# Front of a single-layer S5 + SwiGLU kernel: the modulation rows made in four column pieces at four array positions, their two halves turned one at a time, and the context scaled in two steps around them

## The chip, the cores and the metric

The kernel runs on one core of a Trainium2 chip. The metric is the device time of one execution in microseconds (us), as the median of several runs. TensorE is called PE, VectorE DVE, ScalarE ACT, GpSimd POOL, and SyncE, which here only issues transfers, SP.

## The reference

One layer (kind 0) is computed over 1024 latent tokens with 256 context tokens ahead of them, 1024 channels wide, all in fp32. What matters here stands at its start: the modulation vectors are one row of products with `ada_w`, and the normalised tokens are scaled and shifted by them, those of the context (`c_ctx`) by others than those of the latents (`c`).

```python
m_l = split(silu(c) @ ada_w + ada_b, 6); m_c = split(silu(c_ctx) @ ada_w + ada_b, 6)
h_l = rms_norm(x, norm_mix) * (1 + m_l[1]) + m_l[0]
h_c = rms_norm(ctx, norm_mix) * (1 + m_c[1]) + m_c[0]
y_l = s5_mixer(h_c, h_l, ...)     # 64 groups of 16 channels, complex state of 64, both directions
x = x + m_l[2] * y_l
x = x + m_l[5] * swiglu(modulate(rms_norm(x, norm_ffn), m_l[3], m_l[4]))
out = rms_norm(x, norm_final)
```

## The kernel before, in words

The kernel is written for manual scheduling: every engine runs its instructions in the order in which the Python program issues them, and waits for another engine by semaphores that are put in from the tiles' dependences.

The S5 scan works on chunks of 8 tokens. `U` holds the input as 128 partitions (8 tokens x 16 channels) by 64 groups by 160 columns (32 context chunks `Xc`, 128 latent chunks `X`). For 16 half blocks `hb` (8 groups, one direction each) the program makes a weight matrix, turns it on PE and multiplies U by it:

- `bl_make(hb)` makes the two products of a weight (128x1024 each), on POOL for the `hb` listed in `PMUL`, on DVE for the others; `bl_sum(hb)` adds the two, on POOL for `hb` under 4, and by an accumulating transfer that POOL issues (L433) from 4 on; `bl_tr(hb)` turns the sum in eight PE transposes (L443) and copies the result to the buffer `Win` (L446). `hb` 0 is special: DVE makes both products and their sum, and the copy of its turned weight is shared by ACT (L553) and DVE (L555).
- `sums(hb)` multiplies U by the turned weight (L584) and ACT copies the result into the state buffer (L590 to L593); `pair` and `ctx_tree` combine states on DVE and POOL; `lb_dup` (L331 on PE, L332 on ACT) makes the table `LB` from which the weights are made.
- The modulation (shift and scale) is needed by channel, in the partitions of U. `ada1(h, k)` (L199) adds the products of one 128-row tile of `ada_w` into the PSUM tile `prow`, of half h (512 columns of both shift and scale). `mix_rows` (L456, ACT) copies the rows out, `mix_turn` (L460, PE) turns them, `mix_scale` (DVE, by the helpers on L77 and L80) adds the bias and the norm's weight, `mix_sel` (L475, L476, PE) spreads the result over the partitions, `mix_cols` (L481, ACT) copies it out of PSUM.
- With it `u_act` (L497, ACT, one group an instruction) and `u_lat` (DVE, several groups an instruction) modulate the latent columns and `u_ctx` (POOL, two instructions for 8 groups) the context. Ahead of them `rs_lat` and the product with `rcp` apply the norm on DVE.

Half 0 is handled ahead of the loop over `hb`, half 1 inside it (rows at `hb` 3, scale at `hb` 4). SP loads in a fixed order: x, the context, the first B matrices (`bxy`), then eight tiles of `ada_w` for half 0 and eight for half 1. When the 16 half blocks are through and the context's states are joined, the latent scan runs as a chain of small DVE steps (`scan`, a function of its own), and after it come the GLU and the FFN, which are products on PE.

Of the kernel before, what the change touches and what calls it, by code (L numbers as in the profile page):

```python
# [42 lines left out]
def s5_ffn_kernel(tc, a, out):  # L43
# [3 lines left out]
    with ctx:  # L47
# [23 lines left out]
        def bc(ap, axis, n):  # L71
            sh = list(ap.shape)
            sh.insert(axis, n)
            return ap.unsqueeze(axis).to_broadcast(sh)

        def tt(o, x, y, op, eng=V):
            eng.tensor_tensor(out=o, in0=x, in1=y, op=op)  # L77
# [116 lines left out]

        def ada1(h, *ks):
            for k in ks:
                for b in range(2):
                    i = 2 * b + h
                    PE.matmul(prow[32 * i:32 * i + 2], scs[:, k], stage[h][k][:, b], start=k == 0, stop=k == 7, tile_position=(0, 32 * i))  # L199

        for i in range(10):
            src = X[:, 8 * i:8 * i + 8] if i < 8 else ctxT[:, 32 * i - 256:32 * i - 224]
# [125 lines left out]
        def lb_dup(d, i, pt):  # L328
# [2 lines left out]
            PE.matmul(pt, cid[:, d], CP[:, :, i] if d else CP[:, ::-1, i], start=True, stop=True)  # L331
            S.activation(LB[:, i, :, G * d:G * d + G], pt, AF.Copy, scale=sgn[:, 0:1] if i else 1.0)  # L332

        for i in range(2):
            lb_dup(0, i, pw([512]))
        cmul(PW[:, 7:8], PW[:, 3:4])
        ada1(0, *range(3, 8))
        psW.__exit__(None, None, None)
        psW, pW = pool("psV")

# [64 lines left out]
        def bl_make(hb, o2=None):  # L405

            if hb >= 16:
                return
            b, d = bd(hb)
            es = slice(64 * d + 8 * b, 64 * d + 8 * b + 8)  # L410
            for i in range(2):
                l_ = bc((LBP[hb][:, i] if hb in LBP else LB[:, i, :, es]).rearrange("p s g -> p g s"), 3, HC)
                tt(o2 if i and o2 is not None else bls(hb)[i], bc(BXY[:, b // 2 % 2, i, d, 8 * (b % 2):8 * (b % 2) + 8], 2, T), l_, MUL, E if hb in PMUL else V)
# [38 lines left out]

        r4, mx = view(RA, 74, [4, P]), view(RA, 76, [2, 2, 32])

        def mix_rows():
            S.copy(r4, prow.rearrange("p (m n) -> p m n", m=4))  # L456

        def mix_turn():
            for m in range(4):
                PE.transpose(prow[:, P * m:P * m + P], r4[:, m], ident)  # L460

        def mix_scale(h):

            hs, pt = slice(4 * h, 4 * h + 4), prow.rearrange("p (m n) -> p m n", m=4)
            for r in range(2):
                tt(cb[:, r, :, hs], pt.rearrange("p m (b j q) -> p b j m q", b=2, j=2)[:, :, h, :, r], modb[:, 0:2, hs], ADD)
            stt(cb[:, :, 1, hs], cb[:, :, 1, hs], 1.0, bc(nrm[:, 0, hs], 1, 2), ADD, MUL)
            for r in range(2):
                tt(mx[:, r].rearrange("p b (j g) -> p b j g", g=T), bc(cb[:, r, :, hs], 3, T), bc(bc(msk, 1, 4), 1, 2), MUL)
# [3 lines left out]
        def mix_sel(h):  # L473

            PE.matmul(colp[:, :, 32 * h:32 * h + 32], sel, mx[:, 0], start=True, stop=True)  # L475
            PE.matmul(pcol, sel, mx, start=True, stop=True)  # L476

        def mix_cols(h, eng=V):
            o = cols[:, :, :, 32 * h:32 * h + 32]
            if eng is S:  # L480
                S.copy(o, pcol)  # L481
            else:
                eng.tensor_copy(o, pcol)
# [11 lines left out]
        def u_act(b, n0, n1):  # L495
            for g in range(8 * b + n0, 8 * b + n1):
                S.activation(X[:, g], X[:, g], AF.Identity, bias=cols[:, 0, 0, g:g + 1], scale=cols[:, 0, 1, g:g + 1])  # L497

        def u_lat(b, n0=0):
            gs = slice(8 * b + n0, 8 * b + 8)  # L500
            tt(X[:, gs], X[:, gs], bc(colp[:, 1, gs], 2, P), MUL)
            tt(X[:, gs], X[:, gs], bc(colp[:, 0, gs], 2, P), ADD)
# [36 lines left out]
        lb_psum(0, S)  # L539
        pr0 = pv2()  # L540
        o2 = pr0.rearrange("p j (i s h) -> p (j i) s h", i=4, s=T)
        bl_make(0, o2)
        tt(BL1[0], BL1[0], o2, ADD)
        V.reciprocal(rcp, rsc)
        tt(Xc[:, 0:16], ctxT[:, 0:16], bc(rcp, 1, 16), MUL)
        mix_rows()
        pl1 = pv2()
        lb_dup(1, 0, pl1[:, 0])
        mix_turn()
        mix_scale(0)  # L550
        pt, w_ = bl_tr(0, copy=False)
        mix_sel(0)
        S.copy(w_[:, 0].rearrange("p i n -> p (i n)"), pt[:, 0])  # L553
        mix_cols(0, S)
        V.tensor_copy(w_[:, 1].rearrange("p i n -> p (i n)"), pt[:, 1])  # L555
        u_act(0, 0, 4)
        u_lat(0, 4)
        u_ctx(0)
        lb_dup(1, 1, pl1[:, 1])
        rs_lat(1)  # L560
        bl_tr(1)
# [136 lines left out]
        for hb in range(16):  # L698
            sums(hb)
            ada1(1, *ADA1.get(hb, ()))  # L700
            if hb == 0:
                power8()
            if hb == 3:
                mix_rows()
            for n in BLTR.get(hb, (hb + 2,)):
                if n < 16:
                    bl_tr(n)
            if hb == 3:
                mix_turn()
            if hb == 4:  # L710
                mix_scale(1)
                mix_sel(1)
            if hb in RSL:
                rs_lat(RSL[hb])
            if hb == 4:
                mix_cols(1)
                tq = pA.tile([P, 512], F32, tag="r3", name="tq")
                LQ += [t[:, o_:o_ + 192].rearrange("p (r e) -> p r e", e=G) for t, o_ in ((tq, 0), (tq, 192), (LTb, 256))]
            if hb == 0:
                tt(Xc[:, 16:], ctxT[:, 16:], bc(rcp, 1, G - 16), MUL)  # L720
            if hb == 1:
                powers(0)
            if hb == 2:
                powers(1)
                SY.dma_start(BXY[:, 1], a["bxy"][:, 3])
            if hb in UACT:
                u_act(*UACT[hb])
            if hb in UCTX:
                u_ctx(UCTX[hb])
            if hb >= 1:  # L730
                pair(hb - 1, E if hb - 1 in PPAIR else V)
            if hb == 5:
                powers(2, 3)
            for a_ in CTREE.get(hb, ()):
                ctx_tree(*a_)
            if hb + 6 in (7, 9, 11, 12, 14, 15):
                lb_psum(hb + 6)
            bl_sum(hb + 5)
            bl_make(hb + 6)
            if hb == 3:  # L740
                pw_mul(PW[:, 2:3], PW[:, 0:1], PW[:, 1])
                tt(KD.rearrange("p q g h -> p (q g) h"), bc(pat, 1, 8), bc(dcol, 2, HC), MUL, E)
            if hb == 4:
                pw_mul(PW[:, 4:6], PW[:, 0:2], PW[:, 3])
                pw_mul(PW[:, 6:7], PW[:, 2:3], PW[:, 3])
            if hb in (6, 8):
                pw_full(hb // 2 - 3)
            if hb == 9:
                cs_load(0)
            if hb == 11:  # L750
                V.tensor_copy(LQ[4], SQ[4])
                cs_sign(0)
            for _ in range(CLAT.get(hb, 0)):
                CL0.pop(0)()
            ada_load(ADA2.get(hb, 0))
# [1004 lines left out]
```

## Time and profile before

| | |
|---|---|
| median of 3 runs | 1024.42 us (1023.78 to 1026.05) |
| the profiled execution | 1022.42 us, its span in the trace 1020.6 us |
| granted PE clock, mean | 0.991 |
| busy in the span | PE 961.9, DVE 785.5, POOL 766.5, ACT 436.5 us |

Times in the trace count from the start of the span. A row of the timeline gives the start, the length, the engine, the line of the kernel with its operation, out<-in by the names of the tiles, the shape, how many records of that kind follow each other (xN), and in brackets the idle time of the engine just before with the work that ended it. An fp32 product on PE leaves two records. DVE and ACT records may overlap the one after them by some 0.08 us. Nearly all helpers of DVE and POOL record their work under L77, L80, L84 or L86, so such rows are told apart by tile and shape. A row of the waits gives who waited for whom, the sum in us, how often and the longest.

### The profile page before, as it was taken

The page shows a single profiled execution, that of the slowest core. Times are in us where ns is not written, and L with a number is a line of the kernel's source. Part 1 is how long each engine was busy: PE and PEld are TensorE (multiplying, and loading weights), DVE is VectorE, ACT ScalarE, POOL GpSimd, SP SyncE. Part 2 cuts the span into 40 slices and gives each one's busy share as a digit, 9 for nine tenths or more (in the row PEclk, how much of TensorE's full clock was granted, in tenths as well). Part 3 has the DMA queues.
Part 4 walks back from the last instruction along what each step waited for, and adds up shares of the span by engine and source line. Part 5 has one row for each costly group of instructions (what it writes and reads, how often), then busy time and mean ns, then how long its engine had stood idle before and what let it go on. Part 6 is the DMA issues. An engine that isn't in the chain of part 4 may idle for free. (4 is left out here: it accounts for less than half of the span.)

```text
span 1020.6 us, 18545 instructions
## 1 busy us (share of the span) xinstructions
PE 961.9 (94%) x6988; PEld 771.8 (76%) x6988; DVE 785.5 (77%) x1642; ACT 436.5 (43%) x854; POOL 766.5 (75%) x590
## 2 busy tenths in 40 slices
PE   5987798779999999999999999999999999999996
PEld 1466423668999987878888888888888888888885
DVE  7979799994365777997958768585958778686987
ACT  5477622234454663523334343424343343324337
POOL 5799899991682548979786877778686877777674
PEclk9999999989999999999999999999999999999999
DMA  9764997323612021011212112121212111121205
GB/s 335 276 139 91 298 341 231 91 74 89 227 61 83 2 104 62 22 42 42 83 41 74 39 45 62 42 73 52 73 42 82 39 40 58 42 73 52 73 22 165
DMA packets 48546, 98.95 MB, mean 97 GB/s; under 512 B 4285, under 2 KB 18877, under 8 KB 47177
## 3 DMA queue, kind: packets, MB, share of 16 engines
q1 hardware_dynamic: 43272, 86.64, 25.9%
q0 software_dynamic: 2016, 7.34, 3.8%
q10 hardware_dynamic: 3168, 3.79, 1.1%
q8 instruction: 55, 0.90, 0.4%
q14 instruction: 35, 0.28, 0.1%
HBM read 84.25 MB, written 6.17 MB: 89 GB/s over the span
## 5 line engine op out<-in xcount | busy, mean ns | idle before, releaser
L77 POOL TENSOR_TENSOR c<-rxc,c 128x512 fp32r<-128x512 f32 x128 | 170.0, 1342 | 55.6 <-ACT c L1227 53.7
L1286 PE MATMUL ut<-ra,c 128*128 128x512 f32 x400 | 155.8, 390 | 0.5 <-ACT ra L1227 0.3
L1287 PE MATMUL ut<-ra,c 128*128 128x512 f32 x400 | 155.7, 389 | 0.3 <-DVE ra L77 0.3
L1288 PE MATMUL ut<-ra,c 128*128 128x512 f32 x400 | 155.7, 389 | 0.0
L1227 ACT CAST c<-rxc 128x512 fp32r<-128x512 f32 x128 | 79.0, 622 | 146.4 <-PE xt L1568 51.8
L1568 PE MATMUL xt<-c,c 128*128 128x512 f32 x540 | 129.7, 389 | 0.0
L77 DVE TENSOR_TENSOR ru<-ru,xt 128x1024 f32<-128x1024 f32 x90 | 107.8, 1216 | 12.9 <-PE xt L1568 9.1
L1568 PEld LDWEIGHTS xt<-c,c 128*128 128x128 f32 x540 | 101.4, 188 | 21.0
L77 DVE TENSOR_TENSOR ru<-ut,ru 128x512 f32<-128x512 f32 x98 | 67.2, 686 | 42.4 <-PE ut L1288 36.9
L1286 PEld LDWEIGHTS ut<-ra,c 128*128 128x128 f32 x400 | 75.1, 188 | 16.7 <-ACT ra L1227 0.8
L1287 PEld LDWEIGHTS ut<-ra,c 128*128 128x128 f32 x400 | 75.1, 188 | 16.2 <-issue 0.6
L1288 PEld LDWEIGHTS ut<-ra,c 128*128 128x128 f32 x400 | 75.1, 188 | 15.9 <-POOL c L77 0.3
L77 POOL TENSOR_TENSOR c<-rw,c 128x512 fp32r<-128x512 f32 (+1 forms) x29 | 39.8, 1372 | 37.3 <-ACT c L1227 36.6
L77 POOL TENSOR_TENSOR c<-ru,c 128x512 fp32r<-128x512 f32 (+1 forms) x39 | 58.0, 1487 | 9.3 <-ACT c L1227 4.9
L1288 PE MATMUL ut<-c,c 128*128 128x512 f32 x160 | 62.4, 390 | 1.3 <-POOL c L77 1.3
L1287 PE MATMUL ut<-c,c 128*128 128x512 f32 x160 | 62.3, 389 | 0.0
L1286 PE MATMUL ut<-c,c 128*128 128x512 f32 x160 | 62.2, 389 | 0.0
L77 POOL TENSOR_TENSOR rxc<-rxc 128x512 f32<-128x512 f32 x40 | 60.9, 1523 | 1.6
L1568 PE MATMUL ut<-c,c 128*128 128x512 f32 x216 | 51.9, 389 | 0.0
L584 PE MATMUL pv<-ru,c 128*64 128x160 f32 x512 | 43.7, 312 | 7.3 <-POOL ru L77 2.6
L77 DVE TENSOR_TENSOR pe<-pe,ru 128x256 f32<-128x256 f32 x64 | 27.4, 429 | 29.5 <-ACT pe L1127 17.4
L77 DVE TENSOR_TENSOR ru<-ru,ut 128x512 f32<-128x512 f32 x76 | 47.3, 680 | 0.3
(427 smaller groups left out, 2568.2 us busy)
## 6 DMA issues: line engine op xcount, KB each, us to landing
c<-in_ada_w SPq DMA_DIRECT2D x46, 256.0 KB
rxc<-in_w SPq DMA_DIRECT2D x38, 256.0 KB
rxc<-in_w SPq DMA_DIRECT2D x19, 512.0 KB
ru<-in_w SPq DMA_DIRECT2D x11, 512.0 KB
rw<-in_w SPq DMA_DIRECT2D x11, 512.0 KB
ra<-in_ada_w SPq DMA_DIRECT2D x10, 512.0 KB
ra<-in_ada_w SPq DMA_DIRECT2D x18, 256.0 KB
ru<-in_xT SPq DMA_DIRECT2D x4, 1024.0 KB
```

The source lines that it names most:

```text
L77: eng.tensor_tensor(out=o, in0=x, in1=y, op=op)
L584: PE.matmul(pv[64 * (i % 2):64 * (i % 2) + 64, ri, c0:c0 + 160], w[:, i, 64 * ri:64 * ri + 64], U[:, 8 * b + 4 * j + i], start=True, stop= ...
L1227: S.copy(o[0], x)
L1286: PE.matmul(pu, wh, bh, start=start, stop=False)
L1287: PE.matmul(pu, wh, bl, start=False, stop=False)
L1288: PE.matmul(pu, wl, bh, start=False, stop=stop)
L1568: PE.matmul(pd, w[:, cs_], b, start=j in (1, 2, 4) and n == 0, stop=n == 2, skip_group_check=j not in (1, 2, 4))
```

## The change

Each `ada1` step makes four products of 256 columns at the four column positions of the array, where it made two of 512 columns at two positions; half h of the modulation then lies in columns 256h to 256h + 255 of `prow`, on four rows. So `mix_rows(h)` copies 256 columns and `mix_turn(h)` turns two tiles, where 512 and four were handled for either half. `mix_scale` adds the bias in four instructions of four columns instead of two of eight. The step `ada1(0, 3)` goes ahead of the first `lb_dup`.

Ahead of the loop the order is another one: the reciprocal `rcp` and the context's first 8 groups come before the products of weight 0; the whole modulation of half 0 (rows, turn, scale, spread, copy out, `u_ctx(0)`, `u_act`) comes before `lb_dup(1, 0)` and before the turning of weight 0; the context's groups 8 to 15 are scaled behind `u_act`, and `u_lat(0, 4)` follows them.

```diff
         def ada1(h, *ks):
             for k in ks:
-                for b in range(2):
-                    i = 2 * b + h
-                    PE.matmul(prow[32 * i:32 * i + 2], scs[:, k], stage[h][k][:, b], start=k == 0, stop=k == 7, tile_position=(0, 32 * i))
+                for i in range(4):
+                    b, j = divmod(i, 2)
+                    PE.matmul(prow[32 * i:32 * i + 2, 256 * h:256 * h + 256], scs[:, k], stage[h][k][:, b, 256 * j:256 * j + 256],
+                              start=k == 0, stop=k == 7, tile_position=(0, 32 * i))
...
+        ada1(0, 3)
         for i in range(2):
             lb_dup(0, i, pw([512]))
         cmul(PW[:, 7:8], PW[:, 3:4])
-        ada1(0, *range(3, 8))
+        ada1(0, *range(4, 8))
...
-        def mix_rows():
-            S.copy(r4, prow.rearrange("p (m n) -> p m n", m=4))
+        def mix_rows(h):
+            S.copy(r4[:, 2 * h:2 * h + 2], prow[:, 256 * h:256 * h + 256].rearrange("p (m n) -> p m n", m=2))
-        def mix_turn():
-            for m in range(4):
+        def mix_turn(h):
+            for m in (2 * h, 2 * h + 1):
                 PE.transpose(prow[:, P * m:P * m + P], r4[:, m], ident)
         def mix_scale(h):
-            hs, pt = slice(4 * h, 4 * h + 4), prow.rearrange("p (m n) -> p m n", m=4)
+            hs, pt = slice(4 * h, 4 * h + 4), prow[:, 256 * h:256 * h + 256].rearrange("p (m n) -> p m n", m=2)
             for r in range(2):
-                tt(cb[:, r, :, hs], pt.rearrange("p m (b j q) -> p b j m q", b=2, j=2)[:, :, h, :, r], modb[:, 0:2, hs], ADD)
+                for b in range(2):
+                    tt(cb[:, r, b, hs].rearrange("p (j m) -> p j m", j=2), pt.rearrange("p m (b j q) -> p b j m q", b=2, j=2)[:, b, :, :, r],
+                       modb[:, b, hs].rearrange("p (j m) -> p j m", j=2), ADD)
...
+        V.reciprocal(rcp, rsc)
+        tt(Xc[:, 0:8], ctxT[:, 0:8], bc(rcp, 1, 8), MUL)
         bl_make(0, o2)
         tt(BL1[0], BL1[0], o2, ADD)
-        V.reciprocal(rcp, rsc)
-        tt(Xc[:, 0:16], ctxT[:, 0:16], bc(rcp, 1, 16), MUL)
-        mix_rows()
+        mix_rows(0)
+        mix_turn(0)
+        mix_scale(0)
+        mix_sel(0)
+        mix_cols(0, S)
+        u_ctx(0)
+        u_act(0, 0, 4)
+        tt(Xc[:, 8:16], ctxT[:, 8:16], bc(rcp, 1, 8), MUL)
+        u_lat(0, 4)
         pl1 = pv2()
         lb_dup(1, 0, pl1[:, 0])
-        mix_turn()
-        mix_scale(0)
         pt, w_ = bl_tr(0, copy=False)
-        mix_sel(0)
         S.copy(w_[:, 0].rearrange("p i n -> p (i n)"), pt[:, 0])
-        mix_cols(0, S)
         V.tensor_copy(w_[:, 1].rearrange("p i n -> p (i n)"), pt[:, 1])
-        u_act(0, 0, 4)
-        u_lat(0, 4)
-        u_ctx(0)
         lb_dup(1, 1, pl1[:, 1])
         rs_lat(1)
         bl_tr(1)
```

In the loop, `mix_rows()` and `mix_turn()` at `hb` 3 become `mix_rows(1)` and `mix_turn(1)`.

How the built programs stand there follows for the engines of which the prediction speaks; "waits" names the queues for whose semaphores an instruction waits, DVE its own among them.

On DVE, ahead of the loop, from the sum of weight 0 to the two instructions of `u_lat(0, 4)`, before (`ru` is U, `ltb` holds `rcp` and the spread modulation, `c1` and `c3` hold weights, `pv` is PSUM, `rxa` the context as loaded):

```order
L77 TENSOR_TENSOR c1_64<-c1_64,pv_290 128x1024 [waits DVE_49]
L544 RECIPROCAL ltb_77<-r0_60 128x32
L77 TENSOR_TENSOR ru_62<-rxa_67,ltb_77 128x16x32 [waits DMAHW0_49,DVE_49]
L77 TENSOR_TENSOR ltb_77<-prow_75,r0_60 128x2x4 [waits DVE_49,DMAHW3_49,PE_49,Activation_49]
L77 TENSOR_TENSOR ltb_77<-prow_75,r0_60 128x2x4 [waits DVE_49]
L80 SCALAR_TENSOR_TENSOR ltb_77<-ltb_77,r0_60 128x2x4 [waits DMAHW4_49,DVE_49]
L77 TENSOR_TENSOR ra_61<-ltb_77,r0_60 128x64 [waits DVE_49]
L77 TENSOR_TENSOR ra_61<-ltb_77,r0_60 128x64
L555 COPY c3_66<-pv_309 128x512 [waits DMAHW2_49,Activation_49]
L77 TENSOR_TENSOR ru_62<-ru_62,ltb_77 128x4x128 [waits PE_49]
L77 TENSOR_TENSOR ru_62<-ru_62,ltb_77 128x4x128 [waits DVE_49]
```

And in the changed program, from the same sum on (the reciprocal and the scaling of the context's first 8 groups stand ahead of the two products of weight 0 now):

```order
L77 TENSOR_TENSOR c1_64<-c1_64,pv_306 128x1024 [waits DVE_49]
L77 TENSOR_TENSOR ltb_77<-prow_75,r0_60 128x4 [waits DMAHW3_49,PE_49,Activation_49]
L77 TENSOR_TENSOR ltb_77<-prow_75,r0_60 128x4 [waits DVE_49] x3
L80 SCALAR_TENSOR_TENSOR ltb_77<-ltb_77,r0_60 128x2x4 [waits DMAHW4_49,DVE_49]
L77 TENSOR_TENSOR ra_61<-ltb_77,r0_60 128x64 [waits DVE_49]
L77 TENSOR_TENSOR ra_61<-ltb_77,r0_60 128x64
L77 TENSOR_TENSOR ru_62<-rxa_67,ltb_77 128x8x32 [waits PE_49]
L77 TENSOR_TENSOR ru_62<-ru_62,ltb_77 128x4x128
L77 TENSOR_TENSOR ru_62<-ru_62,ltb_77 128x4x128 [waits DVE_49]
L563 COPY c3_66<-pv_337 128x512 [waits DMAHW2_49,Activation_49]
```

DVE's share of the copy of weight 0 (128x512) moved from ahead of `u_lat(0, 4)` to behind it, and the second half of the context's scaling stands where that copy stood. The copy's wait on ACT is for ACT's share of the same copy (L553, now L562), in both programs.

On ACT, from `lb_psum(0)` to the second `lb_dup(1, ...)`, before:

```order
L426 COPY lbt_78<-c2_65 128x128 [waits Activation_49]
L456 COPY ra_61<-prow_75 128x512 [waits PE_49]
L332 ACTIVATE c2_65<-pv_297 128x8x64 [waits PE_49]
L553 COPY c3_66<-pv_309 128x512 [waits DMAHW2_49,PE_49]
L481 COPY r0_60<-prow_75 128x4x32 [waits DVE_49,PE_49]
L497 ACTIVATE ru_62<-ru_62,r0_60 128x128 [waits Activation_49]
L497 ACTIVATE ru_62<-ru_62,r0_60 128x128 x3
L332 ACTIVATE c2_65<-pv_297,r0_60 128x8x64 [waits PE_49]
```

And in the changed program:

```order
L428 COPY lbt_78<-c2_65 128x128 [waits Activation_49]
L458 COPY ra_61<-prow_75 128x256 [waits PE_49]
L485 COPY r0_60<-prow_75 128x4x32 [waits DVE_49,PE_49]
L501 ACTIVATE ru_62<-ru_62,r0_60 128x128 [waits Activation_49]
L501 ACTIVATE ru_62<-ru_62,r0_60 128x128 x3
L333 ACTIVATE c2_65<-pv_334 128x8x64 [waits PE_49]
L562 COPY c3_66<-pv_337 128x512 [waits DMAHW2_49,PE_49]
L333 ACTIVATE c2_65<-pv_334,r0_60 128x8x64 [waits PE_49]
```

The table's activation (128x8x64) and the copy of weight 0 moved from ahead of `mix_cols` and `u_act` to behind them.

On PE, from the last `ada1` steps of half 0 to the turning of weight 1, before:

```order
L199 MATMUL prow<-ra,r_60 2x512 x4
L331 MATMUL pv<-ra 128x512
L460 MATMUL prow<-r_60,ra 128x128 x4
L443 MATMUL pv<-r_60,c_64 128x128 x8
L475 MATMUL ltb<-ra,r_60 128x2x32
L476 MATMUL prow<-ra,r_60 128x128
L331 MATMUL pv<-ra 128x512
```

And in the changed program:

```order
L199 MATMUL prow<-ra,r_60 2x256 x8
L462 MATMUL prow<-r_60,ra 128x128 x2
L479 MATMUL ltb<-ra,r_60 128x2x32
L480 MATMUL prow<-ra,r_60 128x128
L332 MATMUL pv<-ra 128x512
L445 MATMUL pv<-r_60,c_64 128x128 x8
L332 MATMUL pv<-ra 128x512
```

The turning of weight 0 and the table's product stand behind the spreading products now, so behind DVE's scaling for which those wait.

More of the change, by code (lines that the diff above doesn't have):

```diff
@@ L703, in s5_ffn_kernel @@
             if hb == 3:
-                mix_rows()
+                mix_rows(1)
             for n in BLTR.get(hb, (hb + 2,)):
@@ L708, in s5_ffn_kernel @@
             if hb == 3:
-                mix_turn()
+                mix_turn(1)
             if hb == 4:
```

## The prediction

> **What bounds the kernel now.** I first read the busy time by stage. Columns: stretch and its length, then PE, PE's weight loads, DVE, ACT and POOL busy (records), the granted clock, the share of the DMA engines, GB/s.
>
> ```profile
> 28.66:44.80 16.14, 14.23 (x103) 7.21 (x104) 15.52 (x23) 8.32 (x18) 12.77 (x9) 1.00 0.89 329
> 44.88:101.84 56.96, 48.16 (x480) 35.43 (x477) 50.48 (x117) 41.66 (x92) 55.63 (x62) 0.97 0.55 112
> 127.65:200.00 72.35, 63.43 (x1064) 29.75 (x1056) 72.06 (x403) 19.79 (x42) 69.77 (x46) 0.99 0.72 231
> 300.00:350.00 50.00, 50.00 (x423) 50.00 (x422) 32.68 (x96) 24.39 (x74) 16.51 (x15) 1.00 0.20 64
> ```
>
> The bound changes hands: DVE fills the stretch to 44.8 us (15.52 of 16.14), POOL the next 57 us (55.63 of 56.96), DVE the scan (72.06 of 72.35), PE everything behind it. PE is not the bound where the change works.
>
> Next the waits, of DVE from 9 to 62 us and of POOL from 44.5 to 108 us (who waited for whom, us in all, times, longest); each list is complete.
>
> ```profile
> DVE ltb L77 <- DVE ru L77: 0.2, 1, 0.2
> ...
> POOL c L77 <- DVE c L77: 0.6, 1, 0.6
> POOL c L433 <- POOL c L77: 0.3, 1, 0.3
> ```
>
> So DVE runs from 9 us on with one gap of 0.2 us, and POOL from 44.88 on with one of 0.3. The timeline shows where they meet.
>
> ```profile
> 37.71 2.58 POOL L77 TENSOR_TENSOR ru<-ru,r 128x256 f32<-128x256 f32 x4 [2.28 <-ACT r L481]
> 40.25 4.01 POOL L77 TENSOR_TENSOR c<-c,c 128x1024 f32<-128x1024 f32 x2
> 42.45 2.35 DVE L77 TENSOR_TENSOR c<-c,lbt 128x1024 f32<-128x1024 f32 x2
> 44.88 4.71 POOL L77 TENSOR_TENSOR c<-c,c 128x1024 f32<-128x1024 f32 x2 [0.62 <-DVE c L77]
> ```
>
> DVE's `bl_make(2)` ends at 42.45 + 2.35 = 44.80, and POOL, which had finished `u_ctx` and `bl_make(3)` at 44.26, starts `bl_sum(2)` at 44.88. That is the handover. The other end of POOL's stretch:
>
> ```profile
> 101.84 0.88 POOL L433 DMA_DIRECT2D c<-c  x1
> c<-c POOLq DMA_DIRECT2D x1, 512.0 KB, 7.8
> 109.81 0.96 PE L443 MATMUL pv<-r,c 128*128 128x128 f32 x7 [1.20 <-DMA c<-c]
> 115.04 0.43 DVE L77 TENSOR_TENSOR ltb<-ra,lta 128x256 f32<-128x256 f32 x1 [4.64 <-ACT ra L593]
> 127.65 0.29 DVE L77 TENSOR_TENSOR ltb<-ra,lta 128x128 f32<-128x128 f32 x1
> ```
>
> POOL issues an accumulating transfer at 101.84, it lands 7.8 us later, PE waited 1.20 us for it before it turns that weight, and DVE waited 4.64 us for the states made with it; the scan starts at 127.65. **The chain** is DVE to 44.80, POOL to 101.84, the transfer, PE and ACT, DVE's scan, PE. What moves the end of `bl_make(2)` moves the end of the kernel.
>
> **The change part by part.** *The pieces at four positions* (PE):
>
> ```profile
> 23.11 1.03 PE L199 MATMUL prow<-c,r 128*2 128x512 f32 x4
> 135.36 1.04 PE L531 MATMUL pm<-ra,r 128*2 128x512 f32 x8
> 31.86 0.09 PEld L199 LDWEIGHTS prow<-ra,r 128*2 128x2 f32 x2 [0.34 <-DMA ra<-in_ada_w]
> 33.36 0.59 ACT L456 COPY ra<-prow 128x512 f32<-128x512 f32 x1 [3.41 <-PE prow L199]
> ```
>
> Two products at two positions take 1.03 us from first start to last end; four of the same size at four positions (`ada`, later) take 1.04. So positions run side by side, and a step of four halves should take about half as long. The last tile lands near 31.8 us, so the rows are ready at about 32.4 instead of 33.3, and copy and turning (0.59 for 512 columns, less for 256) are done by 33.5. If the pieces did not run side by side, nothing would come later than now: ready before 35. That matters only if somebody waits, and DVE, which reads the rows next, is not there before 35.1 (below). Worth: **0**. The eight steps of half 1 run in the loop where POOL is the bound: 0.
>
> *DVE up to the scaling:*
>
> ```profile
> 29.64 1.22 DVE L77 TENSOR_TENSOR ru<-ru,ltb 128x1024 f32<-128x1024 f32 x1
> 30.78 1.21 DVE L77 TENSOR_TENSOR c<-c,lbt 128x1024 f32<-128x1024 f32 x1
> 33.17 1.22 DVE L77 TENSOR_TENSOR c<-c,pv 128x1024 f32<-128x1024 f32 x1
> 34.31 0.35 DVE L544 RECIPROCAL ltb<-r 128x32 f32<-128x32 f32 x1
> 34.69 0.69 DVE L77 TENSOR_TENSOR ru<-rxa,ltb 128x512 f32<-128x512 f32 x1
> 35.58 0.38 DVE L77 TENSOR_TENSOR ltb<-prow,r 128x8 f32<-128x8 f32 x2 [0.20 <-DVE ru L77]
> 36.00 0.17 DVE L80 SCALAR_TENSOR_TENSOR ltb<-ltb,r 128x8 f32<-128x8 f32 x1
> 36.21 0.36 DVE L77 TENSOR_TENSOR ra<-ltb,r 128x64 f32<-128x64 f32 x2
> 52.22 0.42 DVE L77 TENSOR_TENSOR lbt<-ra,lta 128x256 f32<-128x256 f32 x1
> ```
>
> `rs_lat(0)` still ends at 30.86. The reciprocal waits for it now: 30.90 to 31.25. The context's first half has 256 elements, for which I take 0.42 from the 128x256 row: to 31.70. The three steps of weight 0 took 30.78 to 34.39, 3.61 us, and overlap what is ahead by 0.08: 31.62 to 35.23. Then the scaling: instructions of four columns are not in the trace; the nearest row is two of eight in 0.38, 0.21 from start to start. I take 0.21 each (bounds: 0.10, if half the columns take half the time, and 0.21, what eight columns take); four make 0.84; with 0.21 and 0.36 behind, from 35.15 to **36.56**. Before it was 36.21 + 0.36 = 36.57, with a gap of 0.20 that goes. So the modulation comes no earlier: half the context moved behind it saves 0.27 us, the gap 0.2, the two added instructions take 0.42 back.
>
> [...]
>
> *From the scaling to `rs_lat(1)`:*
>
> ```profile
> 36.62 0.43 PE L475 MATMUL ltb<-ra,r 128*128 128x64 f32 x2 [0.94 <-DVE ra L77]
> 37.17 1.02 PE L331 MATMUL pv<-ra 128*128 128x512 f32 x2
> 38.03 1.04 PE L443 MATMUL pv<-r,c 128*128 128x128 f32 x8
> 34.41 0.60 ACT L332 ACTIVATE c<-pv 128x512 f32<-128x512 f32 x1 [0.46 <-PE pv L331]
> 35.72 0.59 ACT L553 COPY c<-pv 128x512 f32<-128x512 f32 x1 [0.71 <-PE pv L443]
> 37.37 0.27 ACT L481 COPY r<-prow 128x128 f32<-128x128 f32 x1 [1.07 <-PE prow L476]
> 37.67 1.65 ACT L497 ACTIVATE ru<-ru,r 128x128 f32<-128x128 f32 x4
> 36.48 0.68 DVE L555 COPY c<-pv 128x512 f32<-128x512 f32 x1
> 37.09 1.41 DVE L77 TENSOR_TENSOR ru<-ru,ltb 128x512 f32<-128x512 f32 x2
> ```
>
> Before, DVE's copy (0.68) stood over PE's spreading product (36.62 + 0.43 = 37.05), `u_lat(0, 4)` followed at 37.09 to 38.50, and `rs_lat(1)` began at 38.42. Now:
>
> 1. The context's second half comes first, but waits for the spreading product (the order shows the wait on PE): 37.06 to 37.48. The cover of that wait is gone. `u_lat(0, 4)`: 37.40 to 38.81. That is 0.31 later.
> 2. Then DVE's copy, which waits for ACT's half of it. PE's product and turning (1.02, 1.04, as in the rows) are through near 39.1 and hide. ACT does not: `mix_cols` and `u_act` end at 37.67 + 1.65 = 39.32 as before, and behind them stand now the table (0.60, from 39.23) and the copy (0.59), to about 40.33. DVE's copy runs 40.36 to 41.04, `rs_lat(1)` begins at 40.96.
>
> So 40.96 - 38.42 = **2.5 us later**: 0.3 for the context's half, 1.55 of waiting for ACT, 0.6 for a copy that lay in a shadow. Behind that DVE's instructions to the end of `bl_make(2)` are the same and have no slack: 44.80 becomes 47.3. Queued behind the waiting copy are `rs_lat(1)`, `u_lat(1)` and both `bl_make`; PE's turning of weight 1 waits for it too, hence `sums(0)`.
>
> *POOL.* `u_ctx(0)` starts at 37.65 as now (ACT's `mix_cols` decides), `bl_make(3)` ends at 44.3, and the wait for DVE grows from 0.62 to 3.1 us. `bl_sum(2)` starts at 47.4, 2.5 us late, and POOL's 57 us behind it have nothing to give back. No transfer moves by itself; each follows the engine that issues it.
>
> **The sum:** the execution that was profiled, 1022.42 us (span 1020.6 and 1.8 around it), becomes 1024.9; the median of the runs shown stands 2.0 above it, so I forecast 1024.42 + 2.5 = **1026.9 us**. The shift's own bounds: 2.0 (the four instructions at 0.10, so all that follows 0.44 earlier) to 2.8 (three of ACT's steps without the overlap of 0.08).
>
> **The rivals.**
>
> *Swallowed on the way.* PE wins back up to 4 us in half 1 (eight steps, each half of 1.03), and PE and DVE both wait at the exit (1.20, 4.64). If one of these, not POOL, sets the exit, 1 us or more of the 2.5 is gone: 1024.4 to 1026.3. For it: slack is visible on PE. Against it: both waits are for work that comes from POOL, whose own list of waits is empty.
>
> *Faster: the rows set the pace.* If the path ran through `prow`, the modulation and the context's first sums (ACT's 3.41 us wait for PE, POOL's 2.28 for ACT, are its marks), then the 0.9 us by which the rows are ready sooner and up to 4.1 us for half 1 (eight steps, each half of 1.03) would come off: 1019.4 to 1023.5, say 1021.5. It decides once DVE reaches the scaling before the rows are turned, that is, from 33.5 us instead of 35.1 on. Against it: DVE's only gap there is 0.2 us, on itself.
>
> [...]
>
> *Slower still: the transfers.* The transfer at the exit took 7.8 us, one of the same size at 49.53 us took less:
>
> ```profile
> c<-rxc POOLq DMA_DIRECT2D x1, 512.0 KB, 4.7
> ```
>
> It runs against the later `ada_w` loads. If these come closer to it, up to the difference, 3.1 us, may come on top: 1028 to 1030.
>
> **How the numbers follow.** Forecast 0.58, swallowed 0.24, faster 0.09, slower still 0.09. 0.2% is 2.0 us, about what a measurement of this kernel can tell from no change. Of the forecast's 0.58 I put 0.06 under that bound; with the swallowed case that makes 0.30 for the same, 0.61 for slower, 0.09 for faster. The forecast's own range is 1025.9 to 1027.7 (2.0 to 2.8, and half a us for the medians); 8 in 10 need most of the swallowed case and part of the transfers': 1024.2 to 1028.4.
>
> **What would show it.** Right: DVE idle some 1.5 us ahead of its copy of weight 0, released by ACT's; `bl_make(2)` ending near 47.3; POOL's wait for DVE 3 us instead of 0.6, and the scan's start at 130.2. The `ada1` steps in half the time, with ACT's wait ahead of `mix_rows` shorter by about 0.9, show the first part right whatever the total does. Wrong: a copy on DVE that does not wait for ACT (then 0.9 us late, about 1025.3), or new gaps on POOL behind 47 us while the scan starts at its old time.

## The result, and the profile after

The changed kernel took 1027.18 us in the median of 10 runs (1026.72 to 1028.17), against 1024.43 for the kernel before on the same chip: a ratio of 1.0031, 95% interval 1.0023 to 1.0039, **2.75 us slower**. Measured once more with the experiments below it was 1027.95 against 1023.99, ratio 1.0034 (1.0018 to 1.0050), 3.96 slower. In us the two intervals are 2.4 to 4.0 and 1.8 to 5.1. The forecast was 1026.9. The profiled execution of the changed kernel is the slowest of its 10 runs (1028.17, span 1026.4), that of the kernel before lies 2.0 below its median; so the two traces stand 5.8 us apart, more than the medians.

DVE's timeline of the changed kernel, from the scaling to `bl_make(2)`:

```profile
35.28 0.78 DVE L77 TENSOR_TENSOR ltb<-prow,r 128x4 f32<-128x4 f32 x4
36.09 0.17 DVE L80 SCALAR_TENSOR_TENSOR ltb<-ltb,r 128x8 f32<-128x8 f32 x1
36.30 0.36 DVE L77 TENSOR_TENSOR ra<-ltb,r 128x64 f32<-128x64 f32 x2
37.44 0.42 DVE L77 TENSOR_TENSOR ru<-rxa,ltb 128x256 f32<-128x256 f32 x1 [0.78 <-PE ltb L479]
37.78 1.40 DVE L77 TENSOR_TENSOR ru<-ru,ltb 128x512 f32<-128x512 f32 x2
42.01 0.69 DVE L563 COPY c<-pv 128x512 f32<-128x512 f32 x1 [2.83 <-ACT c L562]
42.62 3.72 DVE L77 TENSOR_TENSOR ru<-ru,ltb 128x1024 f32<-128x1024 f32 x3
...
46.64 2.35 DVE L77 TENSOR_TENSOR c<-c,lbt 128x1024 f32<-128x1024 f32 x2
```

The scaling ends at 36.30 + 0.36 = 36.66 us. Then come the two gaps that were forecast: one for the spreading product (0.78), one for ACT's copy. The second is 2.83 instead of the forecast 1.55, and `bl_make(2)` ends at 46.64 + 2.35 = 48.99 instead of 47.3 (44.80 before). What ACT waited for stands in its timeline:

```profile
32.29 0.37 ACT L458 COPY ra<-prow 128x256 f32<-128x256 f32 x1 [2.38 <-PE prow L199]
...
39.83 0.58 ACT L333 ACTIVATE c<-pv 128x512 f32<-128x512 f32 x1
41.39 0.59 ACT L562 COPY c<-pv 128x512 f32<-128x512 f32 x1 [0.98 <-PE pv L445]
```

ACT was through with the table at 40.41 and stood idle for 0.98 us until PE had turned weight 0. PE's timeline tells why:

```profile
31.61 0.61 PE L199 MATMUL prow<-ra,r 128*2 128x256 f32 x8 [0.70 <-DMA ra<-in_ada_w]
...
36.71 0.69 PE L479 MATMUL ltb<-ra,r 128*128 128x64 f32 x2 [3.56 <-DVE ra L77]
37.20 0.74 PE L480 MATMUL prow<-ra,r 128*128 128x128 f32 x2
37.73 1.91 PE L332 MATMUL pv<-ra 128*128 128x512 f32 x2
39.44 1.91 PE L445 MATMUL pv<-r,c 128*128 128x128 f32 x8
```

After 3.56 us of idle time every product takes 1.6 to 1.9 times what it took before the change: the spreading 0.69 and 0.74 (0.43, 0.44), the table 1.91 (1.02), the turning 1.91 (1.04). It is the clock. The busy time by stage, columns as in the prediction, with the stretches cut where the trace records a change of the clock:

```profile
29.17:32.58 3.41, 1.82 (x28) 0.30 (x20) 3.31 (x5) 1.00 (x3) 3.41 (x2) 1.00 1.04 396
32.58:35.99 3.41, 0.44 (x2) 0.20 (x2) 3.27 (x7) 0.09 (x1) 2.88 (x2) 1.00 1.06 389
35.99:42.82 6.83, 6.11 (x16) 3.64 (x17) 3.12 (x9) 2.98 (x7) 4.35 (x5) 0.50 0.95 351
42.82:46.23 3.41, 3.41 (x41) 2.90 (x40) 3.34 (x3) 2.73 (x5) 2.08 (x2) 1.00 0.02 8
```

The granted clock is 0.50 from 35.99 to 42.82, behind a stretch in which PE was busy 0.44 of 3.41 us. Before the change it was 1.00 through the whole front (until 84 us). POOL, at the handover and at its last transfer but one:

```profile
49.07 4.71 POOL L77 TENSOR_TENSOR c<-c,c 128x1024 f32<-128x1024 f32 x2 [3.23 <-DVE c L77]
106.02 0.88 POOL L435 DMA_DIRECT2D c<-c  x1
```

`bl_sum(2)` starts 4.19 us late, and 57 us later the transfer is issued 4.18 late (101.84 before): POOL gave nothing back. At the exit, the transfer (the last figure is the time to its landing), PE and DVE:

```profile
c<-c POOLq DMA_DIRECT2D x1, 512.0 KB, 8.2
114.32 1.78 PE L445 MATMUL pv<-r,c 128*128 128x128 f32 x8 [1.81 <-DMA c<-c]
120.26 0.43 DVE L77 TENSOR_TENSOR ltb<-ra,lta 128x256 f32<-128x256 f32 x1 [4.63 <-ACT ra L598]
125.86 0.43 DVE L77 TENSOR_TENSOR ltb<-ra,lta 128x256 f32<-128x256 f32 x1 [1.57 <-ACT ra L595]
```

The transfer landed 8.2 us after its issue instead of 7.8. The turning there took 1.78 instead of 1.06, again at half clock (the trace has it from 114.50 to 117.91), and DVE's second wait is 1.57 instead of 1.15. The scan starts 5.66 us late, and at the end the two traces stand 5.8 us apart.

### The profile page after: what moved, and what is told of

Same layout as the page of the kernel before. It is cut to its first block, busy times and chain, and to the rows that moved or that the text cites. A ratio compares the mean times of both kernels' runs of the same rounds, so it can differ in the third digit from the quotient of the medians.

```text
span 1026.4 us, 18667 instructions
## 1 busy us (share of the span) xinstructions
PE 962.4 (94%) x7048; PEld 775.7 (76%) x7048; DVE 788.6 (77%) x1647; ACT 435.8 (42%) x854; POOL 766.3 (75%) x590
## 5 line engine op out<-in xcount | busy, mean ns | idle before, releaser
L77 DVE TENSOR_TENSOR ru<-ru,ut 128x512 f32<-128x512 f32 x76 | 47.3, 680 | 0.3
```

## The experiments

Two theories stood against each other at first. **Order**: the new order makes DVE wait for ACT's copy and takes the shadow from its own, which costs the forecast's 2.5 us; PE's half clock comes on top. **Pieces**: the pieces, the half rows and the added small instructions decide, for better or worse. The table gives all runs; "wait" is DVE's wait for ACT's copy of weight 0, "handover" the start of POOL's `bl_sum(2)`, "scan" the scan's first instruction that writes `ltc`, all in us of the profiled execution. The medians are those of 6 to 12 runs, and the kernel before of the same chip stands beside each.

| run | wait | handover | scan | median | before | ratio, 95% |
|---|---|---|---|---|---|---|
| before | 0 | 44.88 | 127.85 | | | |
| changed | 2.83 | 49.07 | 133.51 | 1027.18 | 1024.43 | 1.0031 (1.0023 to 1.0039) |
| changed, again | 2.82 | 48.85 | 133.01 | 1027.95 | 1023.99 | 1.0034 (1.0018 to 1.0050) |
| pieces alone | 0 | 45.18 | 128.63 | 1024.10 | 1024.47 | 0.9992 (0.9983 to 1.0001) |
| order alone | 1.47 | 46.83 | 129.90 | 1025.69 | 1024.47 | 1.0011 (1.0000 to 1.0022) |
| PE's work early | 1.47 | 47.41 | 132.04 | 1026.57 | 1024.47 | 1.0018 (1.0007 to 1.0029) |
| PE kept warm | 1.47 | 48.12 | 132.55 | 1027.84 | 1024.47 | 1.0032 (1.0021 to 1.0042) |
| PE kept busy | 1.46 | 47.41 | 132.38 | 1028.54 | 1024.63 | 1.0039 (1.0027 to 1.0051) |
| PE kept busy, again | 1.46 | 48.13 | 131.99 | 1029.15 | 1023.99 | 1.0046 (1.0033 to 1.0058) |
| ACT copies both | 0 | 45.62 | 129.62 | 1024.23 | 1024.63 | 0.9997 (0.9988 to 1.0005) |
| ACT copies both, PE busy | 0 | 53.07 | 137.69 | 1028.06 | 1023.99 | 1.0041 (1.0025 to 1.0058) |
| delay in DVE's way | 0 | 47.04 | 130.71 | 1027.06 | 1024.63 | 1.0023 (1.0013 to 1.0034) |
| one sum moved to DVE | 0 | 45.27 | 127.23 | 1021.86 | 1024.63 | 0.9980 (0.9970 to 0.9991) |
| pieces, one sum on DVE | 0 | 45.21 | 128.21 | 1022.59 | 1023.99 | 0.9979 (0.9968 to 0.9991) |

**Pieces alone.** The pieces and half rows with the old order of the front, as a diff against the changed kernel (as all below, where nothing else is said).

```diff
-        ada1(0, 3)
...
-        ada1(0, *range(4, 8))
+        ada1(0, *range(3, 8))
...
         bl_make(0, o2)
         tt(BL1[0], BL1[0], o2, ADD)
+        V.reciprocal(rcp, rsc)
+        tt(Xc[:, 0:16], ctxT[:, 0:16], bc(rcp, 1, 16), MUL)
         mix_rows(0)
+        pl1 = pv2()
+        lb_dup(1, 0, pl1[:, 0])
         mix_turn(0)
         mix_scale(0)
+        pt, w_ = bl_tr(0, copy=False)
         mix_sel(0)
...
```

> Pieces alone: the modulation in four column pieces and half rows, with the old order of everything in the front. Theory (DVE sets the pace, the order costs the time): the pieces bring nothing; the scaling's two added instructions cost the 0.40 us by which four (0.78) took longer than two (0.38) in the traces, and DVE reads the spreading product that much later; bl_make(2) ends at 45.2 us instead of 44.80, the median is 0.4 above the kernel before: 1024.8, within 1024.2 to 1025.4. No wait of DVE for ACT's copy; PE not idle for over 1 us there, its granted clock 1.00 throughout. Rival (the rows set the pace): 0.9 to 5 us faster, 1019.4 to 1023.5.

DVE's and POOL's timelines:

```profile
35.49 0.78 DVE L77 TENSOR_TENSOR ltb<-prow,r 128x4 f32<-128x4 f32 x4 [0.20 <-PE pv L444]
36.79 0.68 DVE L558 COPY c<-pv 128x512 f32<-128x512 f32 x1
45.18 4.71 POOL L77 TENSOR_TENSOR c<-c,c 128x1024 f32<-128x1024 f32 x2 [0.60 <-DVE c L77]
```

The copy of weight 0 stands in its old place without a wait, the handover is 0.30 late. PE stood idle for up to 1.48 us here, and its granted clock was 1.00 from 28.00 to 46.00 us. The median, 0.37 below the kernel before (interval 1.7 below to 0.1 above), is 0.1 under the range and not to be told from no change. The pieces cost next to nothing and bring nothing that can be measured; of the rival's 0.9 to 5 us the medians leave only the lower edge open, and the trace shows nothing that came sooner at the handover.

**Order alone.** Whole rows in two pieces of 512 columns (the old `ada1`, `mix_rows`, `mix_turn`, `mix_scale`), the new order.

```diff
...
-        mix_rows(0)
-        mix_turn(0)
+        mix_rows()
+        mix_turn()
...
```

> Order alone: the new order of the front with the modulation in its old form, two pieces of 512 columns and whole rows. Theory (the order costs the time; PE's slow clock adds to it only after an idle time of some 3 us): PE turns the rows until about 34.8 us and is called for again at about 36.2, 1.4 us of idle, so its clock stays at 1.00; the scaling ends about 36.2; DVE waits 1.3 to 1.7 us for ACT's half of weight 0; rs_lat(1) begins near 40.6 instead of 38.42, bl_make(2) ends near 47.0; median 1026.1 to 1026.9. Rival (the order is free, the pieces and half rows cost the time): 1024.4.

```profile
39.76 0.69 DVE L560 COPY c<-pv 128x512 f32<-128x512 f32 x1 [1.47 <-ACT c L559]
46.83 4.71 POOL L77 TENSOR_TENSOR c<-c,c 128x1024 f32<-128x1024 f32 x2 [3.10 <-DVE c L77]
```

```profile
31.23:34.65 3.42, 2.65 (x14) 0.69 (x10) 3.39 (x4) 0.59 (x1) 3.34 (x3) 1.00 1.03 383
34.65:38.06 3.41, 1.98 (x12) 1.45 (x13) 2.75 (x9) 1.19 (x4) 2.13 (x3) 1.00 1.06 388
```

The wait of DVE is there, 1.47, and with it most of the loss: handover 1.95 late, against 0.30 with the pieces alone. PE's granted clock is 1.00 throughout the front: with the products in two long pieces PE is busy for 2.65 and 1.98 us in the two stretches shown, where it was for 1.82 and 0.44 with the short ones. So the half clock of the changed kernel comes from the pieces and the order together; in these traces neither alone brought it. The "some 3 us" of the expectation was the author's estimate from the changed kernel's 3.56 us: PE's wait of 1.52 us here, with the clock at 1.00, fits it, but in two runs below half clock came behind waits that were shorter than 3 us, 1.51 in the next one and 2.44 where ACT copies both. The median is 1.22 above the kernel before (interval 0.0 to 2.3), 0.4 under the expected range.

**PE's work early.** The changed kernel with the table's product and the turning of weight 0 issued on PE ahead of the spreading products; the other engines as changed.

```diff
         mix_turn(0)
+        pl1 = pv2()
+        p10 = pl1[:, 0].rearrange("p (s g) -> p s g", s=T)
+        PE.matmul(p10, cid[:, 1], CP[:, :, 0], start=True, stop=True)
+        pt, w_ = bl_tr(0, copy=False)
         mix_scale(0)
...
-        pl1 = pv2()
-        lb_dup(1, 0, pl1[:, 0])
-        pt, w_ = bl_tr(0, copy=False)
+        S.activation(LB[:, 0, :, G:2 * G], p10, AF.Copy, scale=1.0)
```

> The changed kernel, with PE's table product and its turning of weight 0 issued ahead of the spreading product as before the change; the order of DVE, ACT and POOL is that of the changed kernel. Theory (ACT's queue costs the 2.5 us that were forecast, and 1.5 us beside them came from PE, which ran at half its clock after 3.56 us of idle and turned weight 0 late): the granted clock stays at 1.00 from 33 to 44 us, DVE's wait for ACT's copy falls from 2.83 to about 1.5, bl_make(2) ends near 47.4 instead of 48.99; median 1.2 to 1.7 below the changed kernel, 1025.5 to 1026.0. Rival (ACT's place in the queue alone, PE's clock does not matter): the wait stays near 2.8 and the median at 1027.2.

```profile
40.35 0.69 DVE L565 COPY c<-pv 128x512 f32<-128x512 f32 x1 [1.47 <-ACT c L564]
47.41 4.71 POOL L77 TENSOR_TENSOR c<-c,c 128x1024 f32<-128x1024 f32 x2 [2.61 <-DVE c L77]
```

With weight 0 turned in time, DVE's wait is 1.47 and the handover at 47.41, which is what the prediction had (1.55 and 47.4). The expectation missed on the clock: it still fell to half, behind the products for which DVE waits (0.67 in the mean from 36.70 to 39.50 us, so half from some 37.7 on, and 0.50 from 39.50 to 43.50). The median is 2.10 above the kernel before, 0.6 over the range: of the 1.66 us gained at the handover the medians show 0.6 against the changed kernel's first, 1.4 against its second.

**PE kept warm.** The changed kernel with 26 turnings of a constant in PE's idle time.

```diff
         mix_turn(0)
+        pl1 = pv2()
+        for i in range(26):
+            PE.transpose(pl1[:, 0, 128 * (i % 4):128 * (i % 4) + 128], ident, ident)
         mix_scale(0)
...
-        pl1 = pv2()
```

> The changed kernel with 26 turnings of a constant into a free bank added on PE, between the turning of the rows and the spreading product, so that PE is not idle; nothing else moved. Theory (idle time lowers PE's clock): granted clock 1.00 where it was 0.50 (36.7 to 41.5 us), spreading products at 0.43 and 0.44 instead of 0.69 and 0.74, weight 0 turned by 39.4 instead of 41.3, DVE's wait for ACT's copy near 1.5, bl_make(2) ends near 47.4; median 1025.5 to 1026.0. Rival (the slow stretch comes from the order of the products or from the transfers beside them, not from idle time): clock 0.50 as in the changed kernel, median 1027.2 or, with the added work in the way, above.

PE's timeline, and the busy time from 33.00 to 36.70:

```profile
32.97 4.67 PE L554 MATMUL pv<-r 128*128 128x128 f32 x26
37.47 0.33 PE L479 MATMUL ltb<-ra,r 128*128 128x64 f32 x2
```

```profile
33.00:36.70 3.70, 3.70 (x21) 3.70 (x20) 3.28 (x9) 0.00 (x0) 2.37 (x1) 0.54 1.05 386
```

This refuted the theory as it was put. PE was busy without a break, and still at half clock: the turnings took 4.67 us and pushed the spreading products to 37.47. The clock of 0.54 makes half clock for some 3.4 of these 3.70 us; from 28.00 to 33.00 and from 36.70 to 46.00 it was 1.00. From 28.00 to 33.00 PE was busy for 3.21 of 5.00 us. So in this trace work on PE did not keep the clock up in the stretch in which it ran, and the half clock stood behind one in which the short pieces, which wait for the loads, had left PE idle for 1.79 us. With the clock at 1.00 again, DVE's wait was 1.47, but behind the late spreading the handover came at 48.12. The median, 1027.84, is 1.8 over the expected range and where the rival had it; that rival's cause is tested by the next run.

**PE kept busy.** Six turnings after each of the steps 4, 5 and 6 of half 0 (18 in all), and 24 in the idle time.

```diff
-        ada1(0, *range(4, 8))
+        pd = pw([512])
+        for k in range(4, 8):
+            ada1(0, k)
+            for i in range(6 if k < 7 else 0):
+                PE.transpose(pd[:, 128 * (i % 4):128 * (i % 4) + 128], ident, ident)
...
         mix_turn(0)
+        pl1 = pv2()
+        for i in range(24):
+            PE.transpose(pl1[:, 0, 128 * (i % 4):128 * (i % 4) + 128], ident, ident)
...
-        pl1 = pv2()
```

> The changed kernel with constants turned on PE, six after each of the pieces' last steps but one, and 24 between the turning of the rows and the spreading product, so that PE is busy from 26 to 36.5 us; nothing else moved. Theory, revised after the runs before (the clock is set anew every 3.41 us by how busy PE was in the 3.41 us before, on a grid that lies otherwise in every execution; the pieces' short steps and the idle time behind them leave PE busy under half of such a stretch): granted clock 1.00 from 26 to 46 us, DVE's wait for ACT's copy at 1.5 instead of 2.83, bl_make(2) ends near 47.4 instead of 48.99; median 0.6 to 1.7 below the changed kernel, 1025.5 to 1026.6. Rival (the clock does not matter for the end): median at 1027.2 or above.

Busy time by stage, and DVE's copy:

```profile
33.20:36.70 3.50, 3.01 (x30) 2.85 (x27) 3.21 (x9) 0.37 (x1) 2.23 (x1) 1.00 1.05 386
36.70:46.00 9.30, 8.36 (x86) 5.59 (x86) 7.19 (x9) 6.31 (x13) 6.39 (x6) 1.00 0.63 231
```

```profile
40.34 0.69 DVE L569 COPY c<-pv 128x512 f32<-128x512 f32 x1 [1.46 <-ACT c L568]
```

In the trace all of it came true: clock 1.00, wait 1.46, handover 47.41. That fits the theory of the clock; one execution does not show the rule. The order of the products and the loads beside them (DMA share 1.05) are those of the changed kernel, so neither makes the slow stretch by itself. The median did not come true: 1028.54 instead of 1025.5 to 1026.6; the profiled execution, 1026.85, is the second fastest of six.

**PE kept busy again, the changed kernel again, and the price of the added turnings.** Three runs on one chip; the third adds the same turnings to the run in which ACT copies both halves (below), where DVE does not depend on PE's turning; its edit beside the one above is

```diff
-        V.tensor_copy(w_[:, 1].rearrange("p i n -> p (i n)"), pt[:, 1])
+        S.copy(w_[:, 1].rearrange("p i n -> p (i n)"), pt[:, 1])
```

> The run with PE kept busy once more, beside the changed kernel itself, since it missed its expectation and had few times. If the price of the clock reaches the end, its median is 0.6 to 1.7 below that of the changed kernel of the same call; if the added turnings cost as much as they save, or the clock in the front does not reach the end, it is level with it or above, by up to 1.4 as in the run before. bl_sum(2) starts at 47.4 either way.

> The changed kernel once more, for a second profile and for times beside the next run. Theory (the grid of 3.41 us lies otherwise in each execution, so the loss in the front differs from one to the next): DVE's wait for ACT's copy between 1.5 and 3.0 us, POOL's bl_sum(2) starts between 47.3 and 49.2; median 1026.7 to 1027.7. Rival (the same loss in each execution): 2.83 and 49.07 again, within 0.3.

> The run in which ACT copies both halves, with the added turnings of constants on PE (18 among the pieces, 24 in the idle time) on top. DVE no longer depends on PE's turning of weight 0 here, so PE's clock in the front hardly matters and the price of the added turnings themselves is seen. Theory A (they cost by themselves what the run with PE kept busy lay above its expectation): bl_sum(2) starts near 45.4 us as without them, but the median is 1.5 to 3 above the kernel before, 1026.1 to 1027.6. Theory B (they cost nothing): median as without them, 1023.7 to 1024.8.

Without the added turnings that kernel was level with the kernel before (0.9997); with them it was 4.07 us above it, more than either theory gave. The added work has a price of its own. DVE's timeline shows part of it, in the run with PE kept busy again and in the one with both:

```profile
33.56 1.23 DVE L77 TENSOR_TENSOR pv<-c,lbt 128x1024 f32<-128x1024 f32 x1 [0.89 <-PE pw L343]
```

```profile
40.64 1.23 DVE L77 TENSOR_TENSOR pv<-c,lbt 128x1024 f32<-128x1024 f32 x1 [1.75 <-PE pw L343]
```

The bank of the first 18 turnings is the one into which DVE makes the second product of weight 0, so DVE now waits for turnings that stand behind loads: 0.89 and 1.75 us here, nothing in the first run's trace. (The execution profiled for the run with both took 1035.51, 7.5 above its median, with the whole front late; only this row is used of it, and its handover and scan in the table are no measure.) The run with PE kept busy again lies 1.20 above the changed kernel beside it, the second case of its expectation, and with that wait its handover came at 48.13 instead of 47.4. So the runs with PE kept busy can't say whether the clock's price at the handover reaches the end. The changed kernel again, DVE and POOL:

```profile
41.78 0.69 DVE L563 COPY c<-pv 128x512 f32<-128x512 f32 x1 [2.82 <-ACT c L562]
48.85 2.38 POOL L77 TENSOR_TENSOR c<-c,c 128x1024 f32<-128x1024 f32 x1 [3.49 <-DVE c L77]
```

Here the rival was right: the same loss again, although the stretch at half clock lay from 35.26 to 42.08 this time (0.50, behind a stretch in which PE was busy for 0.75 of 3.42 us), where it was 35.99 to 42.82; the median is 0.3 over the theory's range. Two executions don't show that it is so wherever the stretches begin.

**ACT copies both.** The changed kernel with DVE's half of the copy given to ACT.

```diff
-        V.tensor_copy(w_[:, 1].rearrange("p i n -> p (i n)"), pt[:, 1])
+        S.copy(w_[:, 1].rearrange("p i n -> p (i n)"), pt[:, 1])
```

> The changed kernel with both halves of weight 0 copied by ACT, so that DVE neither waits for ACT nor copies. Theory (the wait and the uncovered copy are the loss): rs_lat(1) begins near 39.1 us, where u_lat ends, bl_make(2) ends near 45.5 instead of 48.99; POOL's second product of bl_make(3) comes 0.5 later behind the longer ACT, so bl_sum(2) starts between 45.5 and 46.5; median 1025.0 to 1026.0. Rival (the loss lies in the late modulation or in POOL's wait for the tables): bl_sum(2) still near 49, median 1027.2.

```profile
37.74 5.05 DVE L77 TENSOR_TENSOR ru<-ru,ltb 128x512 f32<-128x512 f32 x5
```

```profile
41.58 0.59 ACT L563 COPY c<-pv 128x512 f32<-128x512 f32 x1
45.62 4.73 POOL L77 TENSOR_TENSOR c<-c,c 128x1024 f32<-128x1024 f32 x2 [0.75 <-DVE c L77]
```

`u_lat`, `rs_lat(1)` and `u_lat(1)` run as one block of five without a gap, as before the change. The handover is at 45.62, and the time is that of the kernel before, though the pieces, the new order and PE's half clock (0.51 from 37.20 to 40.60) are all still there. One line takes the whole loss away; the median is 0.8 under the expected range.

**A delay in DVE's way.** The kernel before, with `bl_make(2)` made twice (diff against the kernel before).

```diff
         bl_make(2)
+        bl_make(2)
         bl_sum(2)
```

> The kernel before, with both products of bl_make(2) made twice on DVE (the same values again), which puts 2.27 us in DVE's way and touches neither pieces nor order. Theory (what moves the end of bl_make(2) moves the end of the kernel one for one): bl_sum(2) starts at 47.2 instead of 44.88, scan at 129.9 instead of 127.65, median 1026.2 to 1027.2. Rival (swallowed on the way): median 1024.4 to 1025.7.

```profile
42.35 4.62 DVE L77 TENSOR_TENSOR c<-c,lbt 128x1024 f32<-128x1024 f32 x4
47.04 4.70 POOL L77 TENSOR_TENSOR c<-c,c 128x1024 f32<-128x1024 f32 x2 [2.88 <-DVE c L77]
```

Handover 2.16 late, median 2.43 later (interval 1.3 to 3.5): one for one within the measurement, with no sign that anything is swallowed.

**One sum moved to DVE.** The other direction: the kernel before with `bl_sum(3)` taken from POOL (diff against the kernel before).

```diff
-        bl_sum(3)
...
         bl_make(4)
+        tt(bls(3)[0], bls(3)[0], bls(3)[1], ADD)
         bl_sum(4)
```

> The kernel before, with bl_sum(3) taken from POOL (half of 4.71 us) and done by DVE behind bl_make(4), which DVE does in about 1.14 us. Theory (POOL, without gaps from 44.88 to 101.84 us, sets the pace and DVE has room there): POOL's last two transfers are issued about 2.1 us sooner, the scan starts 1.5 to 2.2 us sooner, median 1022.2 to 1022.9. Rival (DVE's room is used up, or other waits take the place): median 1024.4, or up to 1.1 above.

```profile
45.27 2.38 POOL L77 TENSOR_TENSOR c<-c,c 128x1024 f32<-128x1024 f32 x1 [0.62 <-DVE c L77]
48.38 1.01 POOL L433 DMA_DIRECT2D c<-rxc  x1 [0.73 <-issue]
...
100.68 0.87 POOL L433 DMA_DIRECT2D c<-c  x1
```

POOL's stretch to that transfer is 100.68 - 45.27 = 55.41 us instead of 56.96: of the 2.3 us that the sum took, 0.73 went into a new gap ahead of POOL's first transfer. With the handover 0.39 late the transfer is issued 1.16 sooner and the scan starts 0.62 sooner, less than the 2.1 and 1.5 to 2.2 expected. The median is 2.77 below the kernel before (interval 0.9 to 3.1), 0.3 better than expected; the profiled execution lies 1.86 above it. That POOL sets the pace holds in both directions by the medians; in the trace only 0.62 us of the gain stand at the scan.

**Pieces, with one sum on DVE.** The two edits that did not lose, as a diff against the kernel of the pieces alone:

```diff
-        bl_sum(3)
...
         bl_make(4)
+        tt(bls(3)[0], bls(3)[0], bls(3)[1], ADD)
         bl_sum(4)
```

> The pieces with the old order, and bl_sum(3) moved from POOL to DVE behind bl_make(4): the two edits that did not lose, together. Theory (POOL's stretch is the bound, the pieces cost nothing): bl_sum(2) starts near 45.2, POOL's last two transfers are issued near 100.6 and 104.2, median 2 to 3.2 below the kernel before, 1021.3 to 1022.5. Rival (the gain of the sum on DVE was chance): median 1024.0 to 1024.6.

1022.59, ratio 0.9979 (0.9968 to 0.9991): better than both kernels, level with the sum on DVE alone (0.9980). The gain is the sum's by these medians; it ended 0.1 over the expected range. The one profiled execution (1023.21) doesn't show it, as its scan starts at 128.21.

## Why the prediction was right, point by point

- **The chain** (DVE to `bl_make(2)`, POOL to the transfer, the scan) held: what was put in at the handover (delay) or taken out there (ACT copying both) or from POOL's stretch (sum on DVE) showed in the median within its interval.
- **The pieces are worth 0**: with the old order that is what the pieces alone show (0.37 faster, interval 1.7 faster to 0.1 slower). With the new order they are not free: order alone kept its clock (1.00). A step of eight records takes 0.61 us where one of four took 1.03, ACT's wait ahead of the rows is 2.38 instead of 3.41, and nobody waited for it, as DVE came to the scaling only at 35.28.
- **The scaling's end**: 36.66 against 36.56. The four small instructions took 0.78 against 0.84, so the two added ones cost 0.40 against 0.42.
- **DVE waits for ACT's copy, and its own copy has lost its shadow**: forecast 1.55 and 0.6, measured 1.47 in the runs in which PE had turned the weight in time, with 0.6 for the copy (42.01 to 42.62). ACT copying both shows that these are the loss.
- **The step that was mis-sized**: "PE's product and turning (1.02, 1.04, as in the rows) are through near 39.1 and hide." They took 1.91 each, at half clock, and were through at 41.35. With the late spreading this made the wait 2.83 and the handover 49.07, where the run with PE's work early has 47.41 and the prediction 47.4: 1.66 us. The prediction took durations from rows at full clock for a place where the new order left PE without work for 3.56 us.
- **The sum**: 2.5 forecast, 2.75 and 3.96 measured. That the first median hit to 0.3 us is partly luck, since the handover was 1.7 and 1.5 us later than forecast in the two traces, and the second median is 1.05 over the forecast. In the order alone, without pieces, the clock stays at 1.00 and the median is 1.5 below the changed kernel's first; that fits a price of the clock that reaches the end, but some 0.4 of it are the small instructions and the intervals nearly touch. With PE's work early the median is 0.6 below that first one, and there the intervals overlap. Whether all of the price arrives stays open.
- **The rivals**: swallowed on the way fell with the delay; faster by the rows' pace fell with the pieces alone. Slower by the transfers: the transfer at the exit took 0.4 longer, not up to 3.1. The scan began 84.44 us after the handover instead of 82.97 (84.16 the second time). Of these 1.47 us the turning, which began 0.3 later behind the handover and took 0.7 longer, makes 1.0, and DVE's second wait 0.4. The forecast scan start, 130.2, came 3.1 late, by 1.7 at the handover and these 1.5.

## What to carry to other kernels

Where an order takes work from an idle engine's queue and puts it behind another engine's result, look for who reads that work last: here one copy, split between two engines, tied the engine that set the pace to the slower queue, and giving the whole copy to the other engine undid all of the loss that could be measured. A duration in a trace holds for the clock at which it was taken: the table's product took 1.02 us at a granted clock of 1.00 and 1.91 at 0.50, behind 3.41 us in which PE was busy for 0.44. Before using a PE row for a place behind idle time, look at how busy PE is ahead of that place. An experiment that adds harmless work must be read for the buffers it takes: here the added turnings brought a wait of their own.

## What the runs showed of the hardware

- PE's clock was granted in steps of one length. In the profiles of the kernel before and of the changed kernel every stretch at half clock, but the last one of each, cut off by the kernel's end, lasts 3.41 or 6.83 us. The changes lie on a grid of 3.41 us, which lay otherwise in each of three executions: from the first stretches at half clock (84.06 us before the change, 35.99 in the changed kernel, 35.26 in its second run) it counts back to 2.1, 1.9 and 1.1 us behind the start of the span.
- Cut along that grid, the same two profiles have 7 stretches at full clock between 16 and 250 us with PE busy for a share of 0.13 to 0.39 by the profile's records: each of the 7 was followed by half clock. Of 103 with a share of 0.65 and more none was. In between it went both ways: 2 of 11 were, at 0.47 and 0.61. That the clock of a stretch follows from PE's share in the one before is the author's theory; these counts agree with it, and no run shows which share decides.
- The stretch from the first MEMSET behind the scan to DVE's first CAST, with the same code in both, took 28.55 us in the kernel before, without half clock, and 29.50 in the changed kernel, which has half clock from 233.97 to 237.38 in it. That the place of the grid is what spreads the executions is suggested by such cases, not shown.
